# Seven quarter products in place of eight in most first-layer chunks of three perceptrons, and a new order of chunks

## Chip, cores and metric

The kernel runs on one core of a Trainium2 chip. The metric is the device time of one execution in microseconds (us): 2350.43 us is the median of three runs of the kernel before (2341.58 to 2351.89). The engines are TensorE (PE for its matmuls, PEld for its weight loads), VectorE (DVE), ScalarE (ACT), GpSimd (POOL) and SyncE (SP, which issues DMAs).

## What is computed

512 tokens of width 1024 go through six stages: an RWKV time mix, a perceptron, a forgetting attention, a perceptron, a sparse attention with a convolution branch, a perceptron. The change touches the three perceptrons alone. Each is

```python
def rmsnorm(x, g, eps=NORM_EPS):
    xf = x.astype(jnp.float32)
    y = xf * lax.rsqrt(jnp.mean(xf * xf, axis=-1, keepdims=True) + eps)
    return (y * g.astype(jnp.float32)).astype(x.dtype)

def sq_relu_mlp(h, w_in, w_out):
    return jnp.square(jax.nn.relu(h @ w_in)) @ w_out

x = x + sq_relu_mlp(rmsnorm(x, mlp_norm_g[layer]), mlp_w_in[layer], mlp_w_out[layer])
```

with `w_in` 1024 x 4096 and `w_out` 4096 x 1024, all float32.

## The kernel before

The activations lie with features on partitions and the 512 tokens along the free axis: eight tiles `xs[m]` of 128x512. Every float32 operand of a matmul is split into a high part (a cast to fp32r on ACT) and a low part (the rest, a subtraction on DVE), and each product is three matmuls: high by high, low by high, high by low.

`mlp` (L226 on) works in four quarters of the 4096 hidden features. A quarter has four chunks of `w_in` (256 hidden features each) and then four chunks of `w_out`. A chunk's weights come by `load_w` (L80): two DMAs of 512 KB into `wr` (three buffers), then four casts (L91, ACT) into `wh` and four subtractions (L92, DVE) into `wl`, 512 columns each; `wh` and `wl` have two buffers, so the weights of one chunk can be made while another is in use. `proj_fm` (L137) makes 128 output features with 24 matmuls of 128x512 (eight tiles of the contraction by three, L146, L147, L149) in a PSUM bank `psacc`. A chunk is two of these, 48 matmuls. After each half of an inner chunk ACT takes the relu (L240), DVE multiplies (L241), and `split` (L159, L160) makes `hid` and `hidl`. After each half of an outer chunk DVE multiplies by the squared norm factor into `yt` (L253), and GpSimd (DVE in the last quarter) adds it to `xs[m]` (L254).

The order on each engine is set by the Tile scheduler, which places instructions in one list per engine by its own model of their times; on the chip an engine goes through its list, and an instruction waits on semaphores for what it needs from other engines.

Of the kernel before, what the change touches and what calls it, by code (L numbers as in the profile page):

```python
# [9 lines left out]
F32 = mybir.dt.float32  # L10
F32R = mybir.dt.float32r
I32 = mybir.dt.int32
AF = mybir.ActivationFunctionType
ALU = mybir.AluOpType
# [4 lines left out]
P = 128  # L19
D = 1024  # L20
T = 512
NK = D // P
# [9 lines left out]
class Net:  # L32
# [154 lines left out]
    def sc(self, name):  # L187
        return self.np.tile([P, T], F32, tag="sc", bufs=self.nsc, name=self.nm(name))

    def sqsum(self):  # L190

        nc = self.nc
        acc = self.sc("ssacc")
        for m in range(NK):
            if m == 0:
                nc.scalar.activation(acc, self.xs[m], AF.Square)
            else:
                sq = self.sc("sq")
                nc.scalar.activation(sq, self.xs[m], AF.Square)  # L199
                nc.gpsimd.tensor_tensor(acc, acc, sq, op=ALU.add)  # L200
        return acc

    def rstd(self, acc, square=False, wide=True):
# [21 lines left out]
        nc.scalar.copy(r, pb)  # L225
        return rt, r  # L226

    def mlp(self, gain, w_in, w_out):

        nc, tc = self.nc, self.tc  # L230
        X = self.gained(gain)
        with tc.tile_pool(name=self.nm("mlp"), bufs=2, reuse_waits="tile") as mp:
            for q in range(4):
                H = []
                for cc in range(4):
                    w = self.load_w(w_in[q * 4 + cc], 2048)
                    for mt in range(2):
                        ps = self.proj_fm(w, mt * P, 256, X, range(NK))
                        t = mp.tile([P, T], F32, tag="ht", bufs=4, name=self.nm("ht"))
                        nc.scalar.activation(t, ps, AF.Relu)  # L240
                        nc.vector.tensor_tensor(t, t, ps, op=ALU.mult)  # L241
                        H.append(self.split(mp, t, "hid", 12))
                    if q == 0 and cc == 0:
                        acc = self.sqsum()
                    if q == 0 and cc == 3:
                        _, r2 = self.rstd(acc, square=True)
                for cc in range(4):
                    w = self.load_w(w_out[q * 4 + cc], 2048)
                    for mt in range(2):
                        m = cc * 2 + mt  # L250
                        ps = self.proj_fm(w, mt * P, 256, H, range(NK))
                        t = mp.tile([P, T], F32, tag="yt", bufs=4, name=self.nm("yt"))
                        nc.vector.tensor_tensor(t, ps, r2, op=ALU.mult)  # L253
                        (nc.vector if q == 3 else nc.gpsimd).tensor_tensor(self.xs[m], self.xs[m], t, op=ALU.add)  # L254

    def proj_tm(self, w, X, tt):

# [124 lines left out]
    def fox(self):  # L382
        nc, tc, a = self.nc, self.tc, self.a
        with tc.tile_pool(name="fox", bufs=2, reuse_waits="tile") as fp, \
                tc.tile_pool(name="foxd", bufs=1, space=DRAM) as dp:
            st, X = {}, self.gained()
            acc = self.sqsum()
            H = 16
            f, u, s2, q = [fp.tile([P, 4 * H], F32, name=f"f{n}") for n in "fusq"]
            f3 = f.rearrange("p (t h) -> p t h", h=H)  # L390

            def raws(nm, cc, g):
                wide = nm == "kv_k" and cc == 0
                w = self.load_wide(a[nm][cc], a["kv_f"], H, g) if wide else self.load_w(a[nm][cc], 2048, g)
                raw = fp.tile([P, 1024], F32, tag="raw", bufs=3, name=self.nm("raw"))
# [1275 lines left out]
```

## Time and profile before

| | |
|---|---|
| median of three runs | 2350.43 us |
| the profiled execution: time / span | 2338.97 us / 2337.0 us |
| granted TensorE clock, mean | 0.984 of 2.4 GHz |
| the three perceptrons in the span | 506 to 857, 1135 to 1486, 1985 to 2334 us |
| matmuls | 12545 |

PE busy counts the time in which some matmul is under way; matmuls overlap, since one starts while the one before it still drains, so the time that a matmul adds to a dense stretch is read from the distance of the starts and not from its own duration. A group of instructions lists its line, engine, operation, output and input tiles, shapes, count, busy time and the mean duration of one.

### The profile page before, as it was taken

Reading aid. Unit: us, or ns where it says so; the run is one execution under the profiler, and the core shown is the slowest. Engines: PE = TensorE matmul, PEld = TensorE weight load, DVE = VectorE, ACT = ScalarE, POOL = GpSimd, SP = SyncE. Lnnn points to the kernel's source line nnn. Section 1 sums busy time; section 2 is a strip of 40 time slices with the busy share of each in tenths; the row PEclk is TensorE's granted clock in tenths of the full one; section 3 lists DMA queues with packets and bytes.
Section 4 is the critical chain, followed back from the end, with each engine's and each line's share of the span. In section 5 each row is a group of like instructions: output and inputs, shape, how many; then the busy total and the mean of one; then the engine's idle time right before and its main releaser. Section 6 shows DMA issues by size and latency. Waiting matters only on the chain.

```text
span 2337.0 us, 33070 instructions
## 1 busy us (share of the span) xinstructions
PE 2239.0 (96%) x12545; PEld 1856.5 (79%) x12545; DVE 1367.7 (59%) x2718; ACT 945.0 (40%) x1928; POOL 568.1 (24%) x655
## 2 busy tenths in 40 slices
PE   4988877999999999999999999999999999999999
PEld 4767666778888889987788888897777888888887
DVE  8997778664444467765744444755554445444444
ACT  5575455343322345654523324344334324332331
POOL 6554235221021012444220120303331102012010
PEclk9998888999999999999999999999999999999999
DMA  3158634213232233332323223232223433223322
GB/s 124 39 163 252 176 94 131 65 41 106 90 105 93 92 102 108 98 83 71 104 93 105 91 95 104 75 116 73 84 84 104 135 108 109 90 90 100 99 91 81
DMA packets 104015, 237.37 MB, mean 102 GB/s; under 512 B 9664, under 2 KB 42176, under 8 KB 103856
## 3 DMA queue, kind: packets, MB, share of 16 engines
q1 hardware_dynamic: 73712, 214.28, 28.8%
q10 hardware_dynamic: 30144, 20.98, 3.0%
q8 instruction: 99, 1.62, 0.3%
q14 instruction: 60, 0.49, 0.1%
HBM read 210.02 MB, written 18.91 MB: 98 GB/s over the span
## 4 chain that ended last, share of the span: by engine, by line
PE 82%; DVE 5%; DMA 2%; ACT 1%; issue 1%; POOL 0%; ACTq 0%; SPq 0%; DVEq 0%; POOLq 0%
PE psacc L146 20%; PE psacc L149 20%; PE psacc L147 20%; PE pso L373 2%; PE psacc L268 2%; PE psacc L266 2%; PE psacc L267 2%; PE pst L363 2%; DVE wl L92 1%; PE pso L1447 1%; PE pso L1449 1%; PE pso L1448 1%; DMA xh<-in_x_dram 0%; PE pss L497 0%; PE pss L744 0%
## 5 line engine op out<-in xcount | busy, mean ns | idle before, releaser
L91 ACT CAST wh<-wr 128x512 fp32r<-128x512 f32 (+1 forms) x593 | 324.2, 617 | 470.7 <-PE psacc L149 341.2
L92 DVE TENSOR_TENSOR wl<-wr,wh 128x512 fp32r<-128x512 f32 (+1 forms) x581 | 422.1, 778 | 38.7 <-ACT wh L91 35.8
L146 PE MATMUL psacc<-xg,wh 128*128 128x512 f32 x1104 | 432.6, 392 | 0.0
L147 PE MATMUL psacc<-xg,wl 128*128 128x512 f32 x1104 | 432.1, 391 | 0.0
L149 PE MATMUL psacc<-xgl,wh 128*128 128x512 f32 x1104 | 431.2, 392 | 0.4 <-DVE xgl L176 0.4
L146 PE MATMUL psacc<-hid,wh 128*128 128x512 f32 x768 | 299.7, 393 | 0.0
L149 PE MATMUL psacc<-hidl,wh 128*128 128x512 f32 x768 | 299.1, 392 | 0.0
L147 PE MATMUL psacc<-hid,wl 128*128 128x512 f32 x768 | 298.5, 391 | 0.0
L254 POOL TENSOR_TENSOR xall<-xall,yt 128x512 f32<-128x512 f32 x72 | 107.7, 1495 | 666.3 <-DVE yt L253 666.3
L149 PEld LDWEIGHTS psacc<-xgl,wh 128*128 128x128 f32 x1104 | 207.2, 188 | 44.7 <-DVE xgl L176 1.5
L147 PEld LDWEIGHTS psacc<-xg,wl 128*128 128x128 f32 x1104 | 207.4, 188 | 42.4 <-issue 0.9
L146 PEld LDWEIGHTS psacc<-xg,wh 128*128 128x128 f32 x1104 | 207.4, 188 | 42.2 <-issue 0.5
L253 DVE TENSOR_TENSOR yt<-psacc,rb 128x512 f32<-128x512 f32 x96 | 66.4, 692 | 273.3 <-PE psacc L149 273.3
L241 DVE TENSOR_TENSOR ht<-ht,psacc 128x512 f32<-128x512 f32 x96 | 66.1, 688 | 224.2 <-ACT ht L240 224.0
L240 ACT ACTIVATE ht<-psacc 128x512 f32<-128x512 f32 x96 | 57.6, 600 | 280.2 <-PE psacc L149 280.1
L149 PEld LDWEIGHTS psacc<-hidl,wh 128*128 128x128 f32 x768 | 144.2, 188 | 32.7
L147 PEld LDWEIGHTS psacc<-hid,wl 128*128 128x128 f32 x768 | 144.2, 188 | 32.0
L146 PEld LDWEIGHTS psacc<-hid,wh 128*128 128x128 f32 x768 | 144.2, 188 | 31.5
L266 PE MATMUL psacc<-wh,xg 128*128 128x256 f32 (+2 forms) x504 | 144.3, 287 | 1.7 <-ACT gt L647 1.5
L268 PE MATMUL psacc<-wh,xgl 128*128 128x256 f32 (+2 forms) x504 | 144.0, 286 | 0.6 <-DVE gq L593 0.6
L267 PE MATMUL psacc<-wl,xg 128*128 128x256 f32 (+2 forms) x504 | 144.3, 287 | 0.0
L200 POOL TENSOR_TENSOR ssacc<-ssacc,sq 128x512 f32<-128x512 f32 x35 | 53.0, 1516 | 228.2 <-ACT sq L199 227.2
(492 smaller groups left out, 4067.0 us busy)
## 6 DMA issues: line engine op xcount, KB each, us to landing
wr<-in_mlp_in_dram SPq DMA_DIRECT2D x96, 512.0 KB, 4.2
wr<-in_mlp_out_dram SPq DMA_DIRECT2D x96, 512.0 KB, 4.3
dQ<-q ACTq DMA_DIRECT2D x8, 1024.0 KB, 5.9
wr<-in_w_q_dram SPq DMA_DIRECT2D x12, 512.0 KB, 3.8
wr<-in_rw_k_dram SPq DMA_DIRECT2D x8, 512.0 KB, 3.8
wr<-in_rw_r_dram SPq DMA_DIRECT2D x8, 512.0 KB, 3.3
wr<-in_rw_v_dram SPq DMA_DIRECT2D x8, 512.0 KB, 4.8
wor<-in_rw_o_dram SPq DMA_DIRECT2D x8, 512.0 KB, 3.6
```

The lines of the kernel that those rows point to most:

```text
L91: nc.scalar.copy(h, r)
L92: (eng or nc.vector).tensor_tensor(wl[:rows, b:f], r, h.bitcast(F32), op=ALU.subtract)
L146: nc.tensor.matmul(ps_, wi[0], xh, start=i == 0, stop=False)
L147: nc.tensor.matmul(ps_, wi[1], xh, start=False, stop=False)
L149: nc.tensor.matmul(ps_, wi[0], xl, start=False, stop=i == n - 1)
L240: nc.scalar.activation(t, ps, AF.Relu)
L241: nc.vector.tensor_tensor(t, t, ps, op=ALU.mult)
L253: nc.vector.tensor_tensor(t, ps, r2, op=ALU.mult)
L254: (nc.vector if q == 3 else nc.gpsimd).tensor_tensor(self.xs[m], self.xs[m], t, op=ALU.add)
L266: nc.tensor.matmul(o, xh[:, b], wh, start=kt == 0, stop=False)
L267: nc.tensor.matmul(o, xh[:, b], wl, start=False, stop=False)
L268: nc.tensor.matmul(o, xl[:, b], wh, start=False, stop=kt == NK - 1)
```

## The change

In quarters 1 to 3 of each perceptron (36 of the 48 inner chunks of the kernel) `seven` replaces the plain chunk. The weights of such a chunk are cut in four blocks per pair of contraction tiles, and the tokens in two halves of 256; seven products of quarters, each 4 x 3 matmuls of 128x256, replace eight: 84 matmuls of 128x256 for 48 of 128x512. `load_s` makes three sums of weight blocks besides the blocks (raw parts `sr`, split parts `sw`), `forms` makes two sums of activation quarters per pair once per perceptron (`tf`, `tfl`). One product is written over, and its running value is copied out of PSUM twice (`e0`, `e1`) between accumulations. Squares move from DVE to ACT, the additions to `xs` and `sqsum` from GpSimd to DVE. Quarter `q+1`'s inner chunks are placed among quarter `q`'s outer chunks.

```diff
--- before.py
+++ after.py
@@ -187,7 +187,7 @@
     def sc(self, name):
         return self.np.tile([P, T], F32, tag="sc", bufs=self.nsc, name=self.nm(name))
 
-    def sqsum(self):
+    def sqsum(self, eng=None):
 
         nc = self.nc
         acc = self.sc("ssacc")
@@ -197,7 +197,7 @@
             else:
                 sq = self.sc("sq")
                 nc.scalar.activation(sq, self.xs[m], AF.Square)
-                nc.gpsimd.tensor_tensor(acc, acc, sq, op=ALU.add)
+                (eng or nc.gpsimd).tensor_tensor(acc, acc, sq, op=ALU.add)
         return acc
 
     def rstd(self, acc, square=False, wide=True):
@@ -225,33 +225,150 @@
         nc.scalar.copy(r, pb)
         return rt, r
 
+    def forms(self, mp, gain, p):
+        nc, a, b = self.nc, slice(0, 256), slice(256, 512)
+        (x0, x1), (g0, g1) = self.xs[2 * p:2 * p + 2], [self.v(gain, 2 * p + i) for i in range(2)]
+        t, u, w = self.sc("fd"), self.sc("fu"), self.sc("fw")
+        nc.vector.tensor_tensor(t[:, a], x0[:, b], x0[:, a], op=ALU.subtract)
+        nc.scalar.activation(u[:, a], t[:, a], AF.Copy, scale=g0)
+        nc.scalar.activation(t[:, b], x0[:, b], AF.Copy, scale=g0)
+        for dst, src, sub in ((u[:, b], x1[:, b], u[:, a]), (w[:, a], x1[:, b], t[:, b]),
+                              (w[:, b], x1[:, a], u[:, b])):
+            nc.vector.scalar_tensor_tensor(dst, src, g1, sub, op0=ALU.mult, op1=ALU.subtract)
+        return [self.split(mp, x, "tf", NK) for x in (u, w)]
+    def load_s(self, mp, src):
+        nc = self.nc
+        wh, wl = [self.wp.tile([P, 2048], F32R, tag=t, bufs=2, name=self.nm(t)) for t in ("wh", "wl")]
+        S = [mp.tile([P, 2, T], F32R, tag="sw", bufs=5, name=self.nm("sw")) for _ in range(3)]
+        raws = [self.sc("sr") if i == 1 else mp.tile([P, T], F32, tag="sr", bufs=2, name=self.nm("sr")) for i in range(3)]
+        for s in range(2):
+            raw = self.wp.tile([P, 1024], F32, tag="wr", bufs=3, name=self.nm("wr"))
+            o = 1024 * s
+            nc.sync.dma_start(raw, src[:, o:o + 1024])
+            v = raw.rearrange("p (q k m c) -> p q k m c", q=2, k=2, m=2)
+            a11, a12, a21, a22 = v[:, :, 0, 0], v[:, :, 1, 0], v[:, :, 0, 1], v[:, :, 1, 1]
+            s2, s3, s4 = [x[:, 256 * s:256 * s + 256].rearrange("p (q c) -> p q c", q=2) for x in raws]
+            nc.vector.tensor_tensor(s3, a11, a21, op=ALU.subtract)
+            nc.vector.tensor_tensor(a21, a21, a22, op=ALU.add)
+            nc.vector.tensor_tensor(s2, a21, a11, op=ALU.subtract)
+            nc.vector.tensor_tensor(s4, a12, s2, op=ALU.subtract)
+            for b in range(0, 1024, 512):
+                h, r = wh[:, o + b:o + b + 512], raw[:, b:b + 512]
+                nc.scalar.copy(h, r)
+                nc.vector.tensor_tensor(wl[:, o + b:o + b + 512], r, h.bitcast(F32), op=ALU.subtract)
+        for x, r in zip(S, raws):
+            nc.scalar.copy(x[:, 0], r)
+            nc.vector.tensor_tensor(x[:, 1], r, x[:, 0].bitcast(F32), op=ALU.subtract)
+        return wh, wl, S
     def mlp(self, gain, w_in, w_out):
 
         nc, tc = self.nc, self.tc
         X = self.gained(gain)
         with tc.tile_pool(name=self.nm("mlp"), bufs=2, reuse_waits="tile") as mp:
-            for q in range(4):
-                H = []
-                for cc in range(4):
-                    w = self.load_w(w_in[q * 4 + cc], 2048)
-                    for mt in range(2):
-                        ps = self.proj_fm(w, mt * P, 256, X, range(NK))
-                        t = mp.tile([P, T], F32, tag="ht", bufs=4, name=self.nm("ht"))
-                        nc.scalar.activation(t, ps, AF.Relu)
-                        nc.vector.tensor_tensor(t, t, ps, op=ALU.mult)
-                        H.append(self.split(mp, t, "hid", 12))
-                    if q == 0 and cc == 0:
-                        acc = self.sqsum()
-                    if q == 0 and cc == 3:
-                        _, r2 = self.rstd(acc, square=True)
-                for cc in range(4):
-                    w = self.load_w(w_out[q * 4 + cc], 2048)
-                    for mt in range(2):
-                        m = cc * 2 + mt
-                        ps = self.proj_fm(w, mt * P, 256, H, range(NK))
-                        t = mp.tile([P, T], F32, tag="yt", bufs=4, name=self.nm("yt"))
-                        nc.vector.tensor_tensor(t, ps, r2, op=ALU.mult)
-                        (nc.vector if q == 3 else nc.gpsimd).tensor_tensor(self.xs[m], self.xs[m], t, op=ALU.add)
+            H, F, st = {}, [], {}
+            lo, hi = slice(0, 256), slice(256, 512)
+            def plain(q, cc):
+                w = self.load_w(w_in[q * 4 + cc], 2048)
+                H[q, cc] = []
+                for mt in range(2):
+                    ps = self.proj_fm(w, mt * P, 256, X, range(NK))
+                    t = self.sc("ht")
+                    nc.scalar.activation(t, ps, AF.Relu)
+                    nc.scalar.activation(t, t, AF.Square)
+                    H[q, cc].append(self.split(mp, t, "hid", 12))
+                    yield
+            def seven(q, cc):
+                wh, wl, S = self.load_s(mp, w_in[q * 4 + cc])
+                block = lambda k, m: lambda p: [x[:, 512 * p + 256 * k + 128 * m:][:, :P] for x in (wh, wl)]
+                sums = lambda i: lambda p: [S[i][:, j, 128 * p:128 * p + 128] for j in range(2)]
+                quarter = lambda k, c: lambda p: [x[:, c] for x in X[2 * p + k]]
+                diff = lambda i, c: lambda p: [x[:, c] for x in F[p][i]]
+                def product(ps, A, B, first=True):
+                    for p in range(NK // 2):
+                        (ah, al), (bh, bl) = A(p), B(p)
+                        for i, (x, y) in enumerate(((ah, bh), (al, bh), (ah, bl))):
+                            nc.tensor.matmul(ps, x, y, start=first and p == i == 0, stop=p == 3 and i == 2,
+                                             skip_group_check=not first)
+                A0, B0, C0 = [self.bank(t)[:, lo] for t in ("acc", "t", "o")]
+                t0, t1, e0, e1 = [self.sc("ht") for _ in range(4)]
+                product(A0, block(0, 0), quarter(0, lo))
+                nc.scalar.copy(e0[:, lo], A0)
+                product(C0, block(1, 0), quarter(1, lo))
+                nc.vector.tensor_tensor(t0[:, lo], C0, e0[:, lo], op=ALU.add)
+                nc.scalar.activation(t0[:, lo], t0[:, lo], AF.Relu)
+                product(A0, sums(0), diff(0, hi), first=False)
+                nc.scalar.copy(e0[:, hi], A0)
+                product(B0, sums(1), diff(1, lo))
+                product(A0, block(0, 1), diff(0, lo), first=False)
+                nc.scalar.copy(e1[:, lo], A0)
+                nc.vector.tensor_tensor(t1[:, hi], B0, e1[:, lo], op=ALU.add)
+                yield
+                product(A0, sums(2), quarter(1, hi), first=False)
+                nc.scalar.activation(t0[:, hi], A0, AF.Relu)
+                nc.scalar.activation(t0, t0, AF.Square)
+                H[q, cc] = [self.split(mp, t0, "hid", 12)]
+                product(B0, block(1, 1), diff(1, hi), first=False)
+                nc.vector.tensor_tensor(t1[:, lo], B0, e0[:, hi], op=ALU.add)
+                nc.scalar.activation(t1, t1, AF.Relu)
+                nc.scalar.activation(t1, t1, AF.Square)
+                H[q, cc].append(self.split(mp, t1, "hid", 12))
+                yield
+            def inner(q, cc):
+                return seven(q, cc) if q else plain(q, cc)
+            def outer(q, cc):
+                Hq = [x for c in range(4) for x in H[q, c]]
+                w = self.load_w(w_out[q * 4 + cc], 2048)
+                for mt in range(2):
+                    m = cc * 2 + mt
+                    ps = self.proj_fm(w, mt * P, 256, Hq, range(NK))
+                    t = self.sc("yt")
+                    nc.vector.tensor_tensor(t, ps, st["r2"], op=ALU.mult)
+                    nc.vector.tensor_tensor(self.xs[m], self.xs[m], t, op=ALU.add)
+                    yield
+            def run(*gens):
+                gens = list(gens)
+                while gens:
+                    for g in list(gens):
+                        if next(g, gens) is gens:
+                            gens.remove(g)
+            run(inner(0, 0))
+            acc = self.sqsum(nc.vector)
+            for cc in range(1, 4):
+                F.append(self.forms(mp, gain, cc - 1))
+                run(inner(0, cc))
+            F.append(self.forms(mp, gain, 3))
+            _, st["r2"] = self.rstd(acc, square=True)
+            run(inner(1, 0))
+            for q in range(3):
+                run(outer(q, 0))
+                run(inner(q + 1, 1))
+                run(outer(q, 1))
+                run(outer(q, 2))
+                run(outer(q, 3))
+                run(inner(q + 1, 2))
+                run(inner(q + 1, 3))
+                if q < 2:
+                    run(inner(q + 2, 0))
+            for cc in range(4):
+                run(outer(3, cc))
 
     def proj_tm(self, w, X, tt):
 
```

The lists of the engines, in the first perceptron. On DVE before, around two outer chunks of quarter 1 (`wl` are weights of the chunks to come, `yt` the results of the chunk that PE works on):

```order
L253 TENSOR_TENSOR yt_5785<-psacc_5760,rb_5082 128x512 [waits PE_49,Pool_49]
L253 TENSOR_TENSOR yt_5813<-psacc_5788,rb_5082 128x512 [waits PE_49,Pool_49]
L92 TENSOR_TENSOR wl_5887<-wr_5888,wh_5886 128x512 [waits DMAHW1_49,Activation_49]
L92 TENSOR_TENSOR wl_5887<-wr_5888,wh_5886 128x512 [waits Activation_49]
L92 TENSOR_TENSOR wl_5887<-wr_5894,wh_5886 128x512 [waits DMAHW2_49,Activation_49]
L92 TENSOR_TENSOR wl_5887<-wr_5894,wh_5886 128x512 [waits Activation_49]
L253 TENSOR_TENSOR yt_5855<-psacc_5830,rb_5082 128x512 [waits PE_49,Pool_49]
L253 TENSOR_TENSOR yt_5883<-psacc_5858,rb_5082 128x512 [waits PE_49,Pool_49]
```

On DVE now, where the four outer chunks of quarter 0 end and inner chunk 2 of quarter 1 begins (L340 is the evacuation of the last half of the last outer chunk; L258 to L261 are the weight sums of the inner chunk, L265 its `wl`, and L268, three more rows on, the low parts of the sums):

```order
L340 TENSOR_TENSOR yt_5717<-psacc_5692,rb_5150 128x512 [waits PE_49]
L258 TENSOR_TENSOR sr_5726<-wr_5728 128x256 [waits DMAHW7_49]
L258 TENSOR_TENSOR sr_5726<-wr_5738 128x256 [waits DMAHW0_49]
L341 TENSOR_TENSOR xall<-xall,yt_5717 128x512 [waits DVE_49]
L259 TENSOR_TENSOR wr_5728<-wr_5728 128x2x128 [waits DVE_49]
L259 TENSOR_TENSOR wr_5738<-wr_5738 128x2x128 [waits DVE_49]
L260 TENSOR_TENSOR sr_5725<-wr_5728 128x256 [waits DVE_49]
L260 TENSOR_TENSOR sr_5725<-wr_5738 128x256 [waits DVE_49]
L261 TENSOR_TENSOR sr_5727<-wr_5728,sr_5725 128x256 [waits DVE_49]
L265 TENSOR_TENSOR wl_5721<-wr_5728,wh_5720 128x512 [waits Activation_49]
L261 TENSOR_TENSOR sr_5727<-wr_5738,sr_5725 128x256 [waits DVE_49]
L265 TENSOR_TENSOR wl_5721<-wr_5728,wh_5720 128x512 [waits Activation_49]
```

Before, four L92 for the next chunk stand ahead of the two `yt` of the running chunk; now the first instruction for the next chunk's weights stands behind the `yt` of the running chunk's last half.

On PE now, at the same place (`psacc_5692` is the last half of the last outer chunk, `psacc_5754` and `pso_5756` are the first two products of the inner chunk):

```order
L146 MATMUL psacc_5692<-hid_5107,wh_5650 128x512
L147 MATMUL psacc_5692<-hid_5107,wl_5651 128x512
L149 MATMUL psacc_5692<-hidl_5108,wh_5650 128x512
L302 MATMUL psacc_5754<-xg_4690,wh_5720 128x256 [waits Activation_49]
L302 MATMUL pso_5756<-xg_4694,wh_5720 128x256
L302 MATMUL psacc_5754<-xg_4690,wl_5721 128x256 [waits DVE_49]
```

No matmul of another chunk stands between the last outer matmul and the first that waits for the new weights; that wait is on the first L264 (ACT), which itself waits for the first L259 (DVE).

On ACT now, within the same inner chunk and into the next (L308, L313 and L316 are the copies out of PSUM, L264 the casts of the next chunk's blocks, L267 the casts of its sums, L320 and L321 relu and square of the running chunk):

```order
L308 COPY ht_5759<-psacc_5754 128x256 [waits PE_49]
L311 ACTIVATE ht_5757<-ht_5757 128x256 [waits DVE_49]
L313 COPY ht_5759<-psacc_5754 128x256 [waits PE_49]
L316 COPY ht_5760<-psacc_5754 128x256 [waits PE_49,Activation_49]
L264 CAST wh_5864<-wr_5872 128x512 [waits DMAHW1_49,DVE_49]
L264 CAST wh_5864<-wr_5872 128x512
L320 ACTIVATE ht_5757<-psacc_5754 128x256 [waits PE_49]
L264 CAST wh_5864<-wr_5882 128x512 [waits DMAHW2_49,DVE_49]
L264 CAST wh_5864<-wr_5882 128x512
L267 CAST sw_5866<-sr_5869 128x512 [waits DVE_49]
```

All casts of the next chunk stand behind the third copy (L316), which is taken after five of the seven products; DVE's list has the next chunk's L258 behind the instruction that uses this copy (L317) as well.

## Rows read from the trace of the kernel before

**Rows 1.** The page's first part: busy time, share, instructions of each engine.

```profile
PE 2239.0 (96%) x12545; PEld 1856.5 (79%) x12545; DVE 1367.7 (59%) x2718; ACT 945.0 (40%) x1928; POOL 568.1 (24%) x655
```

**Rows 2.** Busy time by stretch, the three perceptrons; clock, DMA share and GB/s last.

```profile
core 0: us, PE busy (x) PEld busy (x) DVE busy (x) ACT busy (x) POOL busy (x), PEclk, DMA share, GB/s
506.00:857.40 351.40, 351.08 (x1556) 290.53 (x1557) 177.00 (x255) 122.55 (x226) 55.74 (x37) 1.00 0.29 95
1135.00:1485.50 350.50, 350.08 (x1548) 288.36 (x1547) 175.11 (x249) 116.64 (x213) 51.97 (x40) 1.00 0.30 97
1985.00:2334.00 349.00, 347.35 (x1517) 283.18 (x1515) 157.06 (x230) 101.76 (x185) 35.90 (x24) 1.00 0.28 92
```

**Rows 3.** Waits of PE from 506 us on, the longest: us, times, longest.

```profile
PE psacc L266 <- ACT gt L647: 1.5, 1, 1.5
```

**Rows 4.** Timeline of PE, first and last of 78 matmuls in a row: start, us.

```profile
839.72 0.39 PE L146 MATMUL psacc<-hid,wh 128*128 128x512 f32 x1
...
857.18 0.39 PE L149 MATMUL psacc<-hidl,wh 128*128 128x512 f32 x1
```

**Rows 5.** Timeline of PE, first and last of 38 narrow matmuls in a row (attention stage).

```profile
1006.67 0.28 PE L266 MATMUL psacc<-wh,xg 128*128 128x256 f32 x1
...
1011.11 0.28 PE L267 MATMUL psacc<-wl,xg 128*128 128x256 f32 x1
```

**Rows 6.** Groups by line and form, the weight loads of these matmuls.

```profile
L267 PEld LDWEIGHTS psacc<-wl,xg 128*128 128x128 f32 x504 | 95.9, 190 | 1.4 <-issue 0.9
```

**Rows 7.** Timeline of DVE: four subtractions of a chunk's weights in a row.

```profile
608.60 2.49 DVE L92 TENSOR_TENSOR wl<-wr,wh 128x512 fp32r<-128x512 f32 x4
```

**Rows 8.** Timeline of ACT: the four casts of that chunk.

```profile
607.86 2.18 ACT L91 CAST wh<-wr 128x512 fp32r<-128x512 f32 x4
```

**Rows 9.** Groups by line and form on DVE and ACT: count, busy us, mean ns.

```profile
L253 DVE TENSOR_TENSOR yt<-psacc,rb 128x512 f32<-128x512 f32 x96 | 66.4, 692 | 273.3 <-PE psacc L149 273.3
...
L365 DVE COPY pt<-pst 128x256 f32<-128x256 f32 x16 | 6.8, 423 | 13.4 <-PE pst L363 13.2
...
L398 ACT COPY raw<-psacc 128x256 f32<-128x256 f32 x32 | 11.4, 369 | 18.1 <-PE psacc L268 17.9
```

**Rows 10.** Timelines of PE and ACT: a last matmul of a half, then its relu.

```profile
601.50 0.39 PE L149 MATMUL psacc<-xgl,wh 128*128 128x512 f32 x1
...
601.92 0.60 ACT L240 ACTIVATE ht<-psacc 128x512 f32<-128x512 f32 x1 [3.25 <-PE psacc L149]
```

**Rows 11.** Timeline of PE, RWKV stage: a wait and narrow matmuls after it.

```profile
205.73 0.28 PE L268 MATMUL psacc<-wh,xkl 128*128 128x256 f32 x1
207.82 1.35 PE L1247 MATMUL pso<-selr,r 128*128 128x2 f32 x8 [1.82 <-POOL r L1244]
...
209.39 0.41 PE L267 MATMUL psacc<-wl,xk 128*128 128x256 f32 x1
...
210.25 0.41 PE L268 MATMUL psacc<-wh,xkl 128*128 128x256 f32 x1
```

**Rows 12.** Busy time by stretch at that place (columns as in rows 2).

```profile
207.00:208.00 1.00, 0.17 (x2) 0.18 (x2) 1.00 (x1) 0.00 (x0) 0.77 (x1) 1.00 0.59 143
...
209.00:210.00 1.00, 1.00 (x5) 1.00 (x6) 1.00 (x2) 0.00 (x0) 0.41 (x1) 0.50 0.98 235
```

**Rows 13.** DMA issues of the inner chunks' weights: count, KB, us to landing.

```profile
wr<-in_mlp_in_dram SPq DMA_DIRECT2D x96, 512.0 KB, 4.2
```

**Rows 14.** Busy time by stretch: a longer idle stretch, and the clock's return.

```profile
286.00:287.00 1.00, 0.00 (x0) 0.00 (x0) 0.97 (x3) 0.00 (x0) 0.48 (x1) 0.97 0.92 363
287.00:288.00 1.00, 0.09 (x1) 0.09 (x1) 0.93 (x3) 0.59 (x1) 0.00 (x0) 0.50 0.26 98
...
293.00:294.00 1.00, 1.00 (x4) 0.79 (x4) 0.00 (x0) 0.58 (x2) 0.92 (x2) 0.62 0.00 0
294.00:295.00 1.00, 1.00 (x7) 0.87 (x6) 0.00 (x0) 0.48 (x2) 1.00 (x2) 1.00 0.81 184
```

## Prediction

> **What bounds the kernel now.** I read the page's busy times first, then the stretches of the three perceptrons, then PE's waits, then timelines. PE is busy 96% of the span [rows 1]. In the three perceptrons, 1051 us together, it is idle for less than 3 us at the full clock, while DVE is busy about half of the time and ACT a third [rows 2]. From 506 us on the longest wait of PE is 1.5 us, outside the perceptrons [rows 3]. So there PE is the bound, and the other engines lie beside it. What a matmul adds is the distance of the starts: 78 wide ones (128x512) start within 17.46 us, 0.227 us apart [rows 4]; 38 narrow ones (128x256) within 4.44 us, 0.120 us apart [rows 5], a little more than half. In both stretches each matmul has its own weight load.
>
> **What the change removes.** A chunk was 48 x 0.227 = 10.9 us of PE; it becomes 84 x 0.120 = 10.1 us. That is 0.8 us in each of 36 chunks: **29 us less PE work**, if PE is never kept waiting. GpSimd loses its additions, on which PE did not wait.
>
> A rule of the Trainium skill speaks against even this (TensorE: Matmul & The Clock Gate, section Measured speedup vs the span model): a weight load overlaps running matmuls only when it goes to other row groups of the array. The loads here all take the whole array, and by that rule the saving would be a loss. The trace does not bear it out: a load lasts 0.190 us [rows 6] where the starts are 0.120 us apart [rows 5].
>
> **What it adds, and where that lies.** DVE's work for a chunk's weights grows from four wide steps to eight narrow (the sums) and seven wide. In a row a wide step costs 2.49 / 4 = 0.62 us [rows 7], a wide cast on ACT 2.18 / 4 = 0.55 [rows 8]. No row has a narrow subtraction of two SBUF tiles; half of a wide step, 0.31, is one end, the 0.42 of a narrow copy out of PSUM [rows 9] the other, and I take 0.36. A result reaches another engine 0.42 us after the start of its last wide matmul [rows 10], so 0.19 after the next matmul could have started; the lone L340 lasts 0.69 as L253 does [rows 9]. Beside PE this work would be free: 15.7 us of DVE per pair of inner and outer chunk against 21 of PE. But the lists put it behind instructions that wait for PE, so most of it is not beside PE. The places, by kind:
>
> **A, first inner chunk after outer chunks in a row (9 chunks).** DVE's L258 stands behind the L340 that waits for the last outer matmul, and PE's next matmul waits for what follows. Up to the low part of the second sum (third product) DVE does L340, eight narrow and seven wide steps: 0.19 + 0.69 + 8 x 0.36 + 7 x 0.62 = 8.1 us. PE can do only the first two products meanwhile, 24 x 0.12 = 2.9. So 5.2 are idle. Then the second and third copy out of PSUM stand between two products with nothing to put in between: 0.19 + 0.37 [rows 9] + a hop of 0.03, 0.6 each. Together 6.4 x 9 = **58 us** (54 to 62 by the ends of the narrow step).
>
> **B, an inner chunk directly behind another (6).** The next chunk's sums stand behind L317, which waits for the third copy. From there: ten narrow and six wide steps, 7.3 us; PE has two products of the old chunk and two of the new, 48 x 0.12 = 5.8. 1.6 idle, and the two copies: 2.8 x 6 = **17** (14 to 20).
>
> **C, the same start, with outer matmuls behind it (9).** Two wide matmuls and the copies' cover take most: 1.0 x 9 = **9** (0 to 16).
>
> **D, an inner chunk behind an interleaved one (9).** Its sums wait for the outer chunk's last half: L340, eight narrow and six wide steps up to the outer weights, 7.5 us, against 38 narrow and two wide matmuls, 5.0: 2.5 idle. The third copy of this chunk stands on ACT behind four casts for the next outer chunk: 0.19 + 2.18 + 0.4 less one product of 1.4 is 1.3. 3.8 x 9 = **34** (22 to 45).
>
> **E, the first such chunk of a perceptron (3).** The norm factor and the last `forms` stand between the sums on DVE: nearly A, with outer matmuls for the copies. 5.5 x 3 = **17** (9 to 21).
>
> The weights' DMAs land in 4.2 us [rows 13] and are issued a chunk ahead; I cost them at nothing, and the cover is the chunk before. The plain chunks of quarter 0 take DVE's and ACT's extra steps (squares, `sqsum`, `forms`) without a wait: at most ten wide and four narrow steps on DVE, 10 x 0.62 + 4 x 0.36 = 7.6 us, and fourteen on ACT, 14 x 0.55 = 7.7, of the 10.9 that PE takes. If DVE fell behind there, E would grow.
>
> The stalls sum to **135 us** (99 to 164), against 29 gained: +106 (70 to 135).
>
> **The clock.** In A and E PE has nothing at all for 0.19 + 0.69 + three narrow and one wide step + a cast, 3.2 us. In the RWKV stage PE was idle for 1.8 us before a few transposing matmuls [rows 11], the granted clock then went from 1.00 to 0.50 (1.2 GHz) [rows 12], and narrow matmuls started 0.215 apart instead of 0.120 [rows 11]. After a longer idle stretch that ended near 288 us it was back at 1.00 by 294 [rows 14]. At half level the 60 narrow matmuls that A has left after its weights would cost 5.7 us more; but the first five us of such a stretch are bound by weights anyway. I take 1 us for each of 12 places, **12 us** (0 to 36).
>
> The sum against the profiled execution: 2339 - 29 + 135 + 12 = 2457. That execution is 11 us (0.5%) below the median of the runs shown, inside what the terms leave open. Forecast: **2460 us, slower**. Half a per cent, 12 us, is what a measurement of this kernel can tell from no change.
>
> **Rivals.**
> *Faster (0.08).* The weights are always ready, and the 29 us come out: 2339 - 29 = 2310, with the median's offset up to 2321. It needs DVE's list not to hold up PE. For it: DVE and ACT have room on average [rows 2]. Against it: the place of L258 behind a waiting L340, and even with all 15 steps at 0.3 us A would idle 2.5 us and the copies 1.2. It decides where the stalls fall under 0.8 us per chunk, from 135 to 29 in all.
> *No change (0.05).* The interleaved chunks (C, D, E) idle hardly at all, B and A half of what I have: 37 against 29, about 2347 to 2350.
> *The clock decides (0.16).* Every idle stretch of A, D and E brings the half level, and the matmuls behind it pay 3 us or more: 21 places x 3 = 63 in place of 12, 2508. For it: the half level after a wait of 1.8 us, shorter than A's 3.2 [rows 11, 12]. Against it: in D PE is only thinned out, with 40 matmuls in 7.5 us. [...]
> *Loads in the open (0.01).* If the loads of narrow matmuls did not overlap, each would cost 0.12 + 0.19 = 0.31, a chunk 26 us, and the kernel 36 x 15 = 540 more, about 2880. The starts 0.120 us apart speak against it [rows 5, 6].
>
> **The numbers.** Forecast 0.70, clock 0.16, both with the loads case over 0.5% slower: 0.87. Faster 0.08, no change 0.05. The forecast's own ends are 2339 + 70 = 2409 and 2339 + 135 + 36 = 2510; to hold 8 in 10 I take **2390 to 2525**, which has the milder half-way cases below and most of the clock's case above.
>
> **What would show it.** Matmuls rise by 36 x 36 = 1296 to about 13840, PE's busy share falls under 92%, and its waits have DVE (sums and low parts) and ACT (first cast, copies) at the top, some 100 to 160 us, repeating nine times with 5 to 7 us at an A. Narrow matmuls of a product start 0.120 apart. Wrong would be: PE waits under 30 us in all; narrow matmuls further apart than 0.13 at full clock; or the time sitting in quarter 0 or in the stages between the perceptrons.

## The result, and the profile after

The changed kernel takes 2494.68 us, median of 4 runs (2491.98 to 2499.93), against 2346.01 for the kernel before: ratio 1.0636, 95% interval 1.0599 to 1.0673. That is **148.7 us slower**. The forecast was 2460 with a range of 2390 to 2525.

The page's first part, as in [rows 1]:

```profile
PE 2288.4 (92%) x13841; PEld 1936.4 (78%) x13841; DVE 1541.8 (62%) x3291; ACT 1120.1 (45%) x2324; POOL 426.9 (17%) x562
```

1296 matmuls more, as counted, and PE's share falls from 96% to 92%. PE's waits, the largest groups of the new lines and one beside them (us, times, longest):

```profile
PE psacc L302 <- ACT wh L264: 43.0, 19, 3.1
PE psacc L302 <- ACT ht L316: 19.4, 32, 1.2
...
PE psacc L302 <- ACT ht L313: 7.4, 17, 0.5
...
PE psacc L302 <- DVE wl L265: 6.5, 16, 0.8
...
PE pss L223 <- DVE dg L222: 5.3, 4, 1.7
...
PE psacc L146 <- ACT wh L91: 5.1, 10, 0.6
```

These are waits on weights and on copies, in perceptrons that had next to none before [rows 3]. All waits of PE in the three perceptrons come to 93 us (0.4 before), just under the 100 to 160 of the forecast, and to little more than half of the stalls that are counted below (168 us). Two things are missing from them: a wait counts from the modelled end of the matmul before it (3.1 us of a stall of 3.35 at an A), and PE does not count as idle where it runs at the half clock (up to 46 us). The granted clock behind one place A, by stretch (columns as in [rows 2]):

```profile
628.00:631.20 3.20, 0.22 (x1) 0.00 (x0) 2.94 (x8) 0.57 (x2) 0.00 (x0) 1.00 0.00 0
...
634.00:638.00 4.00, 4.00 (x20) 4.00 (x20) 2.51 (x6) 0.74 (x2) 0.00 (x0) 0.50 0.79 265
638.30:644.00 5.70, 4.72 (x37) 4.32 (x37) 0.61 (x3) 1.16 (x3) 0.00 (x0) 1.00 0.00 0
```

PE is empty for three us; then it starts 20 narrow matmuls in 4 us, 0.21 apart, at 0.50; 7 us after it went on it has its full clock back. The same place on DVE and ACT, from their timelines (start, duration, what ended the idle time):

```profile
628.26 0.69 DVE L340 TENSOR_TENSOR yt<-psacc,rb 128x512 f32<-128x512 f32 x1 [4.02 <-PE psacc L149]
628.87 0.75 DVE L258 TENSOR_TENSOR sr<-wr 128x256 f32<-128x256 f32 x2
629.53 0.68 DVE L341 TENSOR_TENSOR xall<-xall,yt 128x512 f32<-128x512 f32 x1
630.13 0.75 DVE L259 TENSOR_TENSOR wr<-wr 128x256 f32<-128x256 f32 x2
...
630.63 2.18 ACT L264 CAST wh<-wr 128x512 fp32r<-128x512 f32 x4 [19.96 <-DVE wr L259]
```

DVE had been idle for 4.0 us and ACT for 20.0 before these rows, and the chunk's two weight DMAs had landed by 612. There was room beside PE and the data was there; L258 did not start, because its place in the list was behind L340.

**Where the time went.** For every matmul of a perceptron I take the distance of its start to the one before it and subtract 0.227 us (wide) or 0.120 (narrow); what is left is summed by the chunk that waits. The last column is the part with a granted clock near the half level.

| place (count) | forecast, us | measured, us | at half level |
|---|---|---|---|
| A (9) | 58 | 70.3 | 26.0 |
| B (6) | 17 | 15.6 | 0 |
| C (9) | 9 | 12.5 | 0 |
| D (9) | 34 | 50.9 | 10.1 |
| E (3) | 17 | 13.7 | 9.8 |
| clock | 12 | (in the rows above) | |
| ahead of E, the norm factor on PE (L222) | 0 | 4.7 | |
| PE work saved, by the distance of the starts | -29 | -29 | |
| stages outside the perceptrons | 0 | 14.8 | |
| sum | 118 | 153 (spans: 2490.3 - 2337.0) | |

By stage, in us of the profiled executions (a perceptron counts from the start of its first matmul to the end of its last; that is a little wider than in [rows 2]):

| kernel | RWKV | attention | sparse attention | the perceptrons | span |
|---|---|---|---|---|---|
| before | 506.9 | 274.3 | 492.0 | 1059.1 | 2337.0 |
| after | 506.3 | 282.5 | 499.3 | 1197.6 | 2490.3 |
| sums with a ring of their own | 505.7 | 304.2 | 497.9 | 1057.0 | 2369.4 |
| plain chunks, new order | 518.4 | 282.1 | 500.6 | 1058.0 | 2363.7 |
| filled waits | 514.6 | 283.7 | 498.5 | 1178.6 | 2480.0 |
| loads one chunk ahead | 511.6 | 282.9 | 499.4 | 1049.3 | 2347.8 |
| yt of the last quarter elsewhere | 519.1 | 275.2 | 491.6 | 1194.7 | 2485.2 |
| loads ahead, yt elsewhere | 509.3 | 275.6 | 491.5 | 1049.2 | 2330.3 |
| the same, old order | 519.5 | 275.6 | 491.6 | 1056.7 | 2348.0 |
| the same, own ring too | 504.2 | 297.7 | 493.0 | 1055.8 | 2355.3 |

The RWKV stage's code is the same in all of them, and its time moves between 504 and 520 us. Its lists do not explain that: in the traces of before, after and experiments 2, 6 and 7 every engine goes through the same instructions of this stage in the same order, and the stage takes 506.9 us before and 518.4 in experiment 2. So one and the same list takes different times in different executions, and where the stage is longer its mean granted clock is lower (columns as in [rows 2]; before, then experiment 2):

```profile
0.00:506.90 506.90, 418.91 (x3160) 343.32 (x3160) 395.34 (x743) 254.05 (x479) 210.82 (x224) 0.93 0.41 124
```

```profile
0.00:518.40 518.40, 428.40 (x3161) 352.09 (x3161) 398.44 (x744) 254.07 (x479) 212.44 (x224) 0.91 0.40 121
```

The profiled executions of experiments 2, 5 and 7, in which it is longest, are also 7 to 9 us above the medians of their kernels. What lengthens it was not tried. So the experiments are read by stage, and a difference of ten us in one execution is not put down to an edit unless its stage shows it.

### The profile page after: what moved, and what is told of

Read it like the earlier page. It is cut to its first block, busy times and chain, and to the rows that moved or that the text cites. A ratio compares the mean times of both kernels' runs of the same rounds, so it can differ in the third digit from the quotient of the medians.

```text
span 2490.3 us, 36449 instructions
## 1 busy us (share of the span) xinstructions
PE 2288.4 (92%) x13841; PEld 1936.4 (78%) x13841; DVE 1541.8 (62%) x3291; ACT 1120.1 (45%) x2324; POOL 426.9 (17%) x562
## 4 chain that ended last, share of the span: by engine, by line
PE 76%; DVE 16%; ACT 3%; DMA 3%; issue 2%; ACTq 0%; POOL 0%; SPq 0%; DVEq 0%; POOLq 0%
PE psacc L146 14%; PE psacc L147 14%; PE psacc L149 14%; PE psacc L302 8%; PE pst L302 3%; PE pso L490 2%; PE psacc L383 2%; PE psacc L385 2%; PE psacc L384 2%; PE pso L302 2%; PE pst L480 2%; DVE wl L265 1%; DVE wl L92 1%; DVE mix L1115 1%; DVE sr L258 1%
## 5 line engine op out<-in xcount | busy, mean ns | idle before, releaser
L92 DVE TENSOR_TENSOR wl<-wr,wh 128x512 fp32r<-128x512 f32 (+2 forms) x437 | 293.8, 714 | 95.1 <-ACT wh L91 92.2
L91 ACT CAST wh<-wr 128x512 fp32r<-128x512 f32 (+1 forms) x449 | 248.2, 615 | 205.7 <-PE psacc L149 152.8
L146 PE MATMUL psacc<-xg,wh 128*128 128x512 f32 x528 | 207.7, 393 | 0.0
L147 PE MATMUL psacc<-xg,wl 128*128 128x512 f32 x528 | 207.7, 394 | 0.0
L149 PE MATMUL psacc<-xgl,wh 128*128 128x512 f32 x528 | 207.2, 393 | 0.0
L264 ACT CAST wh<-wr 128x512 fp32r<-128x512 f32 x144 | 80.9, 616 | 227.9 <-DVE wr L259 227.9
L340 DVE TENSOR_TENSOR yt<-psacc,rb 128x512 f32<-128x512 f32 x96 | 64.8, 688 | 168.0 <-PE psacc L149 168.0
L385 PE MATMUL psacc<-wh,xgl 128*128 128x256 f32 (+2 forms) x504 | 146.0, 290 | 2.5 <-DVE xgl L176 2.5
L317 DVE TENSOR_TENSOR ht<-pst,ht 128x256 f32<-128x256 f32 x36 | 15.2, 423 | 183.8 <-ACT ht L316 183.8
L149 PEld LDWEIGHTS psacc<-xgl,wh 128*128 128x128 f32 x528 | 99.2, 188 | 20.7 <-issue 1.0
L147 PEld LDWEIGHTS psacc<-xg,wl 128*128 128x128 f32 x528 | 99.3, 188 | 20.1 <-issue 0.9
L146 PEld LDWEIGHTS psacc<-xg,wh 128*128 128x128 f32 x528 | 99.2, 188 | 20.0 <-issue 0.5
L383 PEld LDWEIGHTS psacc<-wh,xg 128*128 128x128 f32 x504 | 97.8, 194 | 4.5 <-ACT xg L175 1.8
```

What stands on the lines that cost most here:

```text
L91: nc.scalar.copy(h, r)
L92: (eng or nc.vector).tensor_tensor(wl[:rows, b:f], r, h.bitcast(F32), op=ALU.subtract)
L146: nc.tensor.matmul(ps_, wi[0], xh, start=i == 0, stop=False)
L147: nc.tensor.matmul(ps_, wi[1], xh, start=False, stop=False)
L149: nc.tensor.matmul(ps_, wi[0], xl, start=False, stop=i == n - 1)
L264: nc.scalar.copy(h, r)
```

## The experiments

Two theories stood against each other. **Place:** the work for the weights fits beside PE, but stands too late in the lists. **Amount:** there is too much of it per chunk. A third, **the clock**, asks how much of a wait's price is paid after the wait.

The lists show why L258 is late. Of the three raw sums of a chunk one is taken from the ring `sc`, from which `yt` and the four `ht` of a chunk come too (a ring is the set of buffers that the tiles of one tag take in turn). A ring's tiles are handed out in program order, so the sum cannot be placed before the last `yt` or `ht` of the chunk ahead has been: L340 in A and D, L317 in B.

**1. The sums with a ring of their own.** `sc` gives up one tile, so the memory is the same.

```diff
-        raws = [self.sc("sr") if i == 1 else mp.tile([P, T], F32, tag="sr", bufs=2, name=self.nm("sr")) for i in range(3)]
+        raws = [mp.tile([P, T], F32, tag="sr", bufs=3, name=self.nm("sr")) for i in range(3)]
...
+        n.nsc = 5
         n.np = ctx.enter_context(tc.tile_pool(name="net", bufs=1, reuse_waits="tile"))
```

> One of the three raw sums takes its tile from the ring sc, which the results of the halves (yt) and the four pieces of an inner chunk (ht) use too, and whose tiles are given out in the order of the program. Here the sums have a ring of their own (three tiles; sc has five in place of six, the memory is the same). Theory 1, the place in the list: L258 no longer has to follow the last L340 or L317, so PE's waits for L264 and L265, 49.5 us in the changed kernel, fall under 15 us, the half clock behind the nine long waits goes, and only copies out of PSUM (about 30 us) and the first such chunk of each perceptron (about 14) are left: 2337 - 29 + 44 + 10, about 2365, between 2330 and 2395. Theory 2, the amount of DVE's and ACT's work per chunk: the place changes little, 2450 or more.

Measured: 2371.95 us, ratio to before 1.0109 (1.0094 to 1.0124); 123 us of the 149 are back. DVE's list now has the sums of the chunk behind the outer chunks ahead of the evacuations of the outer chunks before it (`yt_5717` is that of the last half, as ahead of the prediction):

```
L258 TENSOR_TENSOR sr_5726<-wr_5728 128x256
...
L340 TENSOR_TENSOR yt_5619<-psacc_5594,rb_5150 128x512
...
L340 TENSOR_TENSOR yt_5717<-psacc_5692,rb_5150 128x512
```

A falls from 70.3 us to under 4, D from 50.9 to about 4, and B and E are under 4. PE's waits in the first perceptron and at the start of the attention (L385) of this kernel, 506 to 902 us:

```profile
PE psacc L385 <- DVE xgl L172: 4.2, 1, 4.2
PE pss L208 <- DVE ssacc L200: 3.5, 1, 3.5
PE psacc L146 <- ACT wh L91: 1.1, 2, 0.6
PE psacc L302 <- ACT wh L264: 0.9, 2, 0.5
```

Nothing was taken from DVE's or ACT's work, so place it is, and not amount. Most of the copies out of PSUM, for which I had left 30 us, went too: with its weights ready, PE's list has matmuls of the next chunk to put between. In the third perceptron 2.3 us of waits for the third copy (L316) are left. The perceptrons are 2.1 us faster than before and not 29, so 27 us of stalls remain, most of them small: C as it was, and the wait for the norm factor (L208 above) with the half clock behind it. The attention became 22 us longer than after the change; it uses `sc` as well, and `sc` now has five tiles. So the total came near the expected 2365 by two misses that partly cancel: fewer stalls in the perceptrons (27 us for the 44 expected), and 35 us more than before in the other stages where 10 had been added.

**2. The order alone.** All inner chunks plain; order, squares and additions as changed.

```diff
-                return seven(q, cc) if q else plain(q, cc)
+                return plain(q, cc)
...
-                F.append(self.forms(mp, gain, cc - 1))
...
-            F.append(self.forms(mp, gain, 3))
```

> All 48 inner chunks are plain (eight products, 48 matmuls of 128x512), no sums and no forms; the new order of chunks, the squares on ACT and the additions on DVE stay. Theory 1: plain casts wait only for a DMA, so nothing behind L340 holds PE for more than about 1 us: 2335 to 2360, no change against before within about half a per cent. Rival: the alternating order, the squares or the additions cost by themselves, then 2390 or more, and E (the norm factor's chain) shows here too.

Measured: 2359.06 us, 1.0060 (1.0040 to 1.0080). The three perceptrons of this kernel:

```profile
518.40:868.80 350.40, 350.40 (x1555) 290.42 (x1555) 157.68 (x255) 137.42 (x249) 0.00 (x0) 1.00 0.29 95
1150.80:1503.00 352.20, 352.20 (x1554) 290.21 (x1554) 157.54 (x250) 136.13 (x244) 1.69 (x6) 1.00 0.29 96
2003.60:2359.00 355.40, 355.40 (x1554) 290.01 (x1552) 147.58 (x233) 128.57 (x230) 0.00 (x0) 1.00 0.28 93
```

PE has not a gap: 1058.0 us against 1059.1 before. Together the order, the squares on ACT and the additions on DVE cost nothing in the perceptrons. The 14 us lie outside, in the attention and the sparse attention (16, see 5); the longer RWKV stage belongs to the profiled execution, which took 7 us more than the median.

**3. The clock by itself.** The changed kernel with matmuls to spare in the nine waits A.

```diff
-                w = self.load_w(w_out[q * 4 + cc], 2048)
+                w = st["w"] = self.load_w(w_out[q * 4 + cc], 2048)
...
+            def fill(w):
+                ps = self.bank("s")
+                for i in range(13):
+                    nc.tensor.matmul(ps, w[0][:, 256 * 7 + 128:2048], X[i % 8][0], start=i == 0, stop=i == 12)
...
                 run(outer(q, 3))
+                fill(st["w"])
                 run(inner(q + 1, 2))
```

> The changed kernel with 13 more matmuls of 128x512 (2.96 us, into an unused bank, on operands at hand) behind the last outer matmul at each of the nine places A, where PE was idle for 3.2 us. They cost nothing if PE has nothing else to do. Prediction's account: the products behind are bound by their weights for the first five us anyway, so a full clock there gives back 0 to 1.5 us at each place: 2480 to 2495. Rival, the clock decides: the 26 us spent at the half level behind the nine waits come back, 2465 to 2472.

Measured: 2478.79 us, 15.9 less than the changed kernel, between the two forecasts; the perceptrons give back 19.0. From the first narrow matmul of an A to the last of its chunk, the nine places take 130.8 us in the changed kernel and 111.8 here: 2.1 each, the whole 19.0. PE at the place of above, with the last of the added matmuls, and the granted clock there:

```profile
638.04 0.39 PE L347 MATMUL pss<-xg,wh 128*128 128x512 f32 x1
638.57 0.39 PE L302 MATMUL psacc<-xg,wh 128*128 128x256 f32 x1
638.79 0.28 PE L302 MATMUL pso<-xg,wh 128*128 128x256 f32 x1
639.81 0.39 PE L302 MATMUL psacc<-xg,wl 128*128 128x256 f32 x1 [0.74 <-DVE wl L265]
640.03 0.28 PE L302 MATMUL psacc<-xgl,wh 128*128 128x256 f32 x1
640.15 0.28 PE L302 MATMUL psacc<-xg,wh 128*128 128x256 f32 x1
```

```profile
638.00:643.00 5.00, 4.12 (x27) 3.16 (x25) 5.00 (x11) 3.79 (x8) 0.00 (x0) 1.00 0.25 66
```

The narrow matmuls now start 0.120 apart as soon as their weights are there. So the clock cost 2.1 us of the 7.8 at an A, some 19 in all; the other 7 of the 26 us counted at the half level would have been waits on weights at either clock.

**4. Each load one chunk ahead.** Every chunk's generator stops after its load; the loop starts the next chunk's before it runs this one. `plain` and `outer` get the same `yield`. The ring stays.

```diff
                 wh, wl, S = self.load_s(mp, w_in[q * 4 + cc])
+                yield
...
+            for n, g in enumerate(seq):
+                if n + 1 < len(seq):
+                    next(seq[n + 1])
...
+                run(g)
```

> Each chunk's load (DMAs, sums, casts, low parts) is written one chunk earlier in the program, the ring sc as in the changed kernel; L258 of a chunk behind outer chunks then stands behind the third last L340 in place of the last. Theory 1: the nine waits A go (7.8 us each, 70 in all, less the copies), B and D shrink as well: 2360 to 2420. Theory 2: 2450 or more.

Measured: 2346.79 us, 1.0009 (0.9999 to 1.0019): no difference to before, and lower than I had thought. A is gone, of B one copy out of PSUM is left (0.62 us a chunk), D is at about 10 us, C at about 12, E under 2. The perceptrons take 1049.3 us, 9.8 less than before.

**5. The yt of the last quarter from another ring**, on the changed kernel.

```diff
-                    t = self.sc("yt")
+                    t = mp.tile([P, T], F32, tag="sr", bufs=2, name=self.nm("yt")) if q == 3 else self.sc("yt")
```

> The changed kernel, but the yt of the last quarter take their tiles from the ring sr, which is free by then, in place of sc. The squares of the next stage (L199) take sc tiles too, and stand behind the last yt in the program. Theory: this alone puts the six squares and GpSimd's additions behind the end of the perceptron, where they hold up ACT's and DVE's weights; with yt elsewhere the attention and the sparse attention get back 6 to 8 us each: 2478 to 2484, the perceptrons unchanged at 1198. Rival: those 15 us are the scheduler's other choices in these stages: 2490 or more.

Measured: 2480.24 us, 14.4 less than the changed kernel. The attention goes from 282.5 to 275.2 us and the sparse attention from 499.3 to 491.6, back to before (274.3 and 492.0); the RWKV stage, which this edit does not touch, is 12.8 longer in the profiled execution. The mechanism stands in ACT's and DVE's timelines at the start of the attention. In the changed kernel:

```profile
902.45 3.22 ACT L199 ACTIVATE sq<-xall 128x512 f32<-128x512 f32 x6
905.57 2.89 ACT L95 ACTIVATE wh<-wr,vec 128x256 fp32r<-128x256 f32 x7
...
906.10 7.82 DVE L96 SCALAR_TENSOR_TENSOR wl<-wr,vec,wh 128x256 fp32r<-128x256 f32 x7 [2.88 <-ACT wh L95]
913.84 0.68 DVE L172 TENSOR_TENSOR xgl<-xall,xg 128x512 fp32r<-128x512 f32 x1
...
903.14 9.71 POOL L200 TENSOR_TENSOR ssacc<-ssacc,sq 128x512 f32<-128x512 f32 x7 [413.66 <-ACT sq L199]
```

With this edit:

```profile
913.68 3.31 ACT L95 ACTIVATE wh<-wr,vec 128x256 fp32r<-128x256 f32 x8 [2.58 <-issue]
...
916.10 2.06 DVE L96 SCALAR_TENSOR_TENSOR wl<-wr,vec,wh 128x256 fp32r<-128x256 f32 x5
918.08 0.68 DVE L172 TENSOR_TENSOR xgl<-xall,xg 128x512 fp32r<-128x512 f32 x1
```

The attention's squares are `sc` tiles as well, and so had to follow the perceptron's last `yt`. They then held up the casts of the weights on ACT by 3.2 us, and GpSimd's additions ran at the same time as DVE's L96.

**6. Both (4 and 5).** No new lines.

> Both edits: each load written one chunk ahead, and the yt of the last quarter in the ring sr. Theory: the two add up, 2347 - 13 to 15: 2330 to 2337, below the kernel before (2345) by about half a per cent; what is left of the 29 us are stalls of some 20 us in the perceptrons. Rival: the list orders itself anew in the RWKV stage or elsewhere and takes it back: 2340 to 2350.

Measured: 2335.17 us, ratio to before 0.9962 (0.9947 to 0.9977): **faster than both kernels**, than the one before by 0.4%. The first row of its page, and the place A on DVE, ACT and PE (its line numbers are two or three higher: L343 is L340, L304 is L302):

```profile
PE 2217.3 (95%) x13841; PEld 1895.1 (81%) x13841; DVE 1545.5 (66%) x3291; ACT 1118.8 (48%) x2324; POOL 430.4 (18%) x562
```

```profile
611.03 0.75 DVE L258 TENSOR_TENSOR sr<-wr 128x256 f32<-128x256 f32 x2
...
616.73 0.68 DVE L343 TENSOR_TENSOR yt<-psacc,rb 128x512 f32<-128x512 f32 x1
617.33 1.88 DVE L268 TENSOR_TENSOR sw<-sr,sw 128x512 fp32r<-128x512 f32 x3
...
612.80 2.18 ACT L264 CAST wh<-wr 128x512 fp32r<-128x512 f32 x4 [6.51 <-DVE wr L259]
...
620.65 0.39 PE L149 MATMUL psacc<-hidl,wh 128*128 128x512 f32 x1
620.88 0.28 PE L304 MATMUL psacc<-xg,wh 128*128 128x256 f32 x1
620.99 0.28 PE L304 MATMUL psacc<-xg,wl 128*128 128x256 f32 x1
```

The sums are done by 615 and the last low part by 619.2; at 620.88 the first narrow matmul starts 0.23 behind the last wide one, without a wait, and goes on 0.12 apart. DVE's and ACT's busy times are within 4 us of those of the changed kernel.

**7. The same with the old order of chunks**, four inner, then four outer.

```diff
-            seq = [inner(0, c) for c in range(4)] + [inner(1, 0)]
...
+            seq = [f(q, c) for q in range(4) for f in (inner, outer) for c in range(4)]
```

> As the one before, but the chunks in the old order: four inner, then four outer chunks of each quarter. Theory of room: four seven-product chunks in a row ask of DVE 8 x 0.36 + 9 x 0.62 + about 1.7, some 10.2 us for each 10.1 us of PE, so DVE has no slack left and weights come late by 1 to 3 us per chunk from the second on: 20 to 80 us more, 2350 to 2410. Rival, order does not matter once loads are ahead: within 6 us of the one before.

Measured: 2340.49 us, 0.9980 (0.9969 to 0.9991). The theory of room fails: the perceptrons take 1056.7 us, 7.5 more than in 6 and not 20 to 80. Even four such chunks in a row leave DVE just about time. Against before, the chunks of seven products alone are worth a little (2.4 us in the perceptrons); the alternating order is worth some 7 us more.

**8. Both, and the sums in a ring of their own.**

> Loads one chunk ahead, yt of the last quarter in the ring sr, and all three raw sums in that ring too (three tiles; sc has five). Theory: the sums wait for nothing of the running chunk any more, so stalls in the perceptrons fall from about 20 us to 10 to 15: 2322 to 2335. Rival: with five sc tiles the chunk's four pieces and the evacuations hold each other up, or other stages (which use sc as well) get longer, as they did with the ring alone (1308 us against 1294): 2340 to 2360.

Measured: 2362.07 us, 1.0077 (1.0059 to 1.0095). The expected 2322 to 2335 was wrong, the rival right: the perceptrons did not get faster (1055.8 against 1049.2), and the attention, with five tiles in `sc`, is 22 us longer, as in 1.

## Why the prediction came out as it did

**What held.** The bound, the sign and the size: PE work fell by what the spacing of starts gives, and the loss came from DVE's list. The working of A is borne out: idle from 627.83 + 0.23 to 631.30, 3.24 us, where the sum of steps gave 3.2. A pair of narrow sums takes 0.75 us, 0.375 each, for the 0.36 chosen. The third copy of an interleaved chunk costs 1.31 to 1.38 in the first two perceptrons (forecast 1.3; 0.62 in the third). B and C are within 4 us of theirs, and so is E, but only with the 9.8 us at the half level that its sum did not have. Quarter 0 has no stall, and the narrow matmuls start 0.120 apart at the full clock; their loads, 0.19 us each, overlap, so the case of loads in the open is out. (The rule of the Trainium skill that the prediction sets against this stands in that page's section The mechanism, not in the one it names.)

**The clock, 12 us, was too small: it cost between 19 and 39.** The step "I take 1 us for each of 12 places" priced an A at 1 us, since its first five us would be bound by weights anyway. Experiment 3 measured 2.1; without it an A costs 5.7, where I had 6.4. D and E hold another 20 us at the half level, and the fall came in five of the nine D, which I had left out because PE is only thinned out there; in three of the five it is not (see D below). How much of those 20 would have been waits in any case was not tried; 19 and 39 are the two ends. The rival "the clock decides" (63, at 3 us in 21 places) was too high. The clock fell behind all nine A, to 0.50 after 3.1 us of idle time. The price depends on what else the matmuls behind would have waited for.

**D, 34 us, measured 50.9.** The step that failed most is the cover, "against 38 narrow and two wide matmuls, 5.0". I read it from the first perceptron's lists and took it for all three. In the third the outer chunk's matmuls stand alone ahead of D, so that each of its three D begins like an A:

```profile
2151.71 0.40 PE L149 MATMUL psacc<-hidl,wh 128*128 128x512 f32 x1
2155.19 0.39 PE L302 MATMUL psacc<-xg,wh 128*128 128x256 f32 x1 [3.08 <-ACT wh L264]
```

A D costs about 7.4 us there and about 4.5 in the first two perceptrons, for the 3.8 forecast. The half level is in these figures, 10.1 in all. The rest: I let the weights of the outer chunk finish after all of the inner ones, while on DVE and ACT they alternate (L264, L91, L264 and L265, L92, L265). PE's list has both chunks' first matmuls woven together, so it waits at each change: 1.54 us, 0.70 and 0.28 at the first D of the first perceptron.

**The stages outside, 0 us, measured 14.8.** I named time there as a sign that I was wrong, and it is a tenth of the loss. The diff moves `yt` into `sc`; I read that as a change of memory and not of order. Experiment 5 shows 7.3 and 7.7 us of it.

**What I did not see at all** is why L258 stands where it does. I took its place from the list as given; it came from a shared ring, and one line undoes it (experiment 1). The forecast did not need that; the way to a faster kernel did.

**Faster (0.08)** asked for stalls of under 29 us. With the loads ahead, stalls of some 20 us are left (C 12, D 10), and the perceptrons are 9.9 us faster than before out of the 29. That the copies would cost some 30 us in any case (27 in the changed kernel's waits above) was wrong as well: with weights at hand most are covered, and in experiment 6 PE's waits for the third copy are

```profile
PE psacc L304 <- ACT ht L318: 4.6, 10, 0.5
```

## What to carry to other kernels

Where work beside the bound engine turns into waits, ask first for its place in the list, and then what put it there: a tile from a ring shared with the results of the running chunk pins the next chunk's first instruction behind them, though no data flows between the two. Price an idle stretch of PE by what follows it too: here 2 us of 8 came after the wait. Where a stage occurs several times, read the list of each: three of the nine D were not what the first perceptron showed. Before a longer stage is put down to the scheduler, compare its lists. And look at stages that a diff does not name when it takes tiles from a ring that they use.

## What the runs showed of the hardware

**DVE beside GpSimd.** At the start of the attention in the changed kernel, seven L96 (scale and subtract, two inputs in SBUF) take 7.82 us while GpSimd adds (L200, 1.29 to 1.36 us each): five of them last 1.35 to 1.52 us, the last two, when GpSimd's additions are done, 0.47. In experiment 5, where the additions come earlier, five take 2.06 us, 0.48 each. One of the long rows runs from 907.37 to 908.89, beside an addition from 907.24 to 908.60; it and the other four each end 0.28 to 0.29 us behind an addition, as if they had stood still beside it. The Trainium skill (SBUF — State Buffer, section SBUF: two separate sides) says that DVE and GpSimd share a pair of ports that one of them holds for a whole instruction, when a DVE instruction has two inputs in SBUF, while the other waits. These rows agree. Additions that look free on an idle GpSimd made these DVE steps three times as long; whether the sums on GpSimd would have helped or hurt was not tried.
